# An fp32 trunk of two layers: the first steps of the MLPs' second products accumulate a sum on a copied PSUM bank, with a third bank in an opening and three order ties

## The chip, the cores and the metric

The kernel runs on one core of one Trainium2 chip. The metric is the device time of one execution, in microseconds (us), and the median of several runs stands for a kernel. The engines go by the profile's names: PE multiplies matrices, PEld loads PE's weights, DVE is the vector engine, ACT the scalar engine, POOL is GpSimd, and SP is the engine whose queue issues the DMAs. A lower time is better. The granted clock of PE was 1.000 in the profiled execution.

## The reference

The model is two layers over 1024 positions of width 1024. Layer 0 mixes positions with a chunked gating MLP, layer 1 with dilated attention. A dense MLP with a squared ReLU follows each mixer, and it is the two MLPs that the change touches:

```python
def reference(x, ...):
    h = x
    for layer in range(DEPTH):          # DEPTH = 2
        y = _rms_norm(h, mix_norm_g[layer])
        ...
            y = _chunk_gating_mixer(...)            # layer 0
        ...
            y = _dilated_attention_mixer(...)       # layer 1
        h = h + y
        y = _rms_norm(h, mlp_norm_g[layer])
        h = h + jnp.square(jax.nn.relu(y @ w_up[layer])) @ w_down[layer]
    return _rms_norm(h, final_norm_g)
```

`w_up` is 1024 x 4096 and `w_down` 4096 x 1024, all in float32.

## The kernel before

**Precision.** Each fp32 operand is split into two parts, hi and lo. `split` issues the hi part as an ACT copy (line 228) and the lo part as a DVE subtraction (line 229). A product of one block is three matmuls of 512 columns: hi by hi, hi by lo, lo by hi.

**Seven products.** Most MLP work goes as a two by two scheme with seven products instead of eight: sums and differences of the four quarters of the weights (POOL, lines 392 to 397, from four loaded quarters) meet sums and differences of the activations. They are numbered 1 to 7. A product may accumulate on what a PSUM bank already holds (the last argument `True` of `product`).

**Banks.** PSUM has eight banks in two pools: three `mm` banks (`mm_bank()`) and five `at` banks (`at_bank()`). A pool hands its banks out in turn, and a new use waits until the bank's last reader is done.

**Order.** PE's order is the order of the program. A scheduler orders the other engines' instructions by estimated times; `tc.issue_after(x)` around an instruction is a tie, which makes it come after `x` in that order. `more()` takes the next step of preparing the weights that come next.

**An MLP, in order.**

- `mlp` starts with a plain part for the first two column groups (`q` = 0, 1): for each half `s` of the positions, four tiles `n` each accumulate on a bank of their own over eight blocks. When a half is done, ACT empties the four banks with ReLU (line 863) and squares them (line 864).
- `opening` does `q` = 2 to 4 with the seven products, then come `q` = 5 to 15 in a form that copies a bank to another (`sums`) and accumulates there. Terms of the hidden activations go to DRAM (`hid`) in `kept`.
- `Down.run` does the second product in 18 steps `t`. Step `t` has 1, 2, 3 and then 4 blocks in each of its seven products, so 3, 6, 9 or 12 matmuls in each product for t = 0 to 3. `inputs` loads the hidden terms of the step after. `add` adds a finished bank to the residual `h` on DVE (line 1094). `self.u[a]` is the sum that several quarters need; it is kept until its last use in steps 14 to 17, where POOL adds it to `h`.
- In steps `t` < 4 ACT copies the first product's bank `a_` to SBUF as `u` (line 1112), the product 6 goes to an at bank `b`, and DVE adds it to `u` (line 1129). In the steps after that ACT copies `a_` to a second mm bank `sums` (line 1117), product 6 accumulates there, and DVE adds `sums` to `u` (line 1129).
- `Down.early` loads and splits the terms of the last column group, called in the step `q` = 15 of the first product.

**Layer 0 to layer 1.** `begin_attention` calls `value_weights(0)` for the attention's first value weights (line 1204) once layer 0's down product has emptied its last bank.

**The norm's terms.** `Terms.first` makes the normed blocks of the first half of the positions, `keep` (line 435), and `Terms.second` makes those of the second half (`r`, line 454) with differences to the first (`b`, lines 458 and 459). POOL writes two more in place (lines 460 and 461). `there[k]` is the event after which the planner may begin `second` for `k`.

Of the kernel before, what the change touches and what calls it, by code (L numbers as in the profile page):

```python
# [14 lines left out]
AF = mybir.ActivationFunctionType  # L15
ALU = mybir.AluOpType
# [113 lines left out]
def trunk(ctx: ExitStack, tc: tile.TileContext, xT, w_u, w_v, w_o, w_s, b_s, w_qkv, w_vt, w_bo, rel,  # L130
          w_up, w_dn, w_dl, vecs, gain, onehot, outT, outL):
    nc = tc.nc
# [12 lines left out]
    def temp():  # L145
        return tpool.tile([P, HALF], F32, tag="t", name="t")

    def spare():
        return tpool.tile([P, HALF], F32, tag="b", name="b", bufs=2)
# [41 lines left out]
    def mm_bank():  # L191
        return psm.tile([P, HALF], F32, tag="mm", name="mm")

    def at_bank():
        return psa.tile([P, HALF], F32, tag="at", name="at")
# [53 lines left out]

    KCOLS = [blk(k) for k in range(KT)]  # L250

    roots, scaled_by = [], []

    def rsqrt(src, scale, out=None, power_of=True):

# [104 lines left out]
    SEVEN = (1, 5, 7, 6, 2, 3, 4)  # L360
# [6 lines left out]
    def product(bank, w, xs, more=False):  # L367

        for k, x in enumerate(xs):
            three(bank, w, blk(k), x, not more and k == 0, k == len(xs) - 1, skip_group_check=True)  # L370
            flow.pump()
# [44 lines left out]
    class Terms:  # L416
# [25 lines left out]
        def second(self, sq, gi):  # L442
            yield from sq.sums()
            r = sq.rms()
            yield LAT["rms"]
            pb = spread(r)
            tt = nc.vector.tensor_tensor
            for k in range(4):
                yield self.there[k], 0
                y, x, (y0, y1) = [], [], (self.kept[k][:, j, :] for j in range(2))  # L450
                for j in range(2):
                    o = 4 * j + k
                    t = raw()
                    nc.vector.scalar_tensor_tensor(t, h[o][:, sq.cols], vec[:, gi, o:o + 1], pb, op0=ALU.mult, op1=ALU.mult)  # L454
                    y.append(t)
                    x.append(pair().split(t))
                t1, t2 = spare(), spare()
                tt(t1, y[0], y0, op=ALU.subtract)
                tt(t2, y[1], t1, op=ALU.subtract)
                nc.gpsimd.tensor_tensor(y0, y[1], y[0], op=ALU.subtract)  # L460
                nc.gpsimd.tensor_tensor(y1, y1, t2, op=ALU.subtract)
                yield 2 * LAT["tile"]
                for j in range(2):
                    self.blocks[j, 1].append(x[j])
                self.t[5].append(pair("t1").split(t1))
                self.t[6].append(pair("t2").split(t2))
# [279 lines left out]
    for gi, chunks in enumerate(((0, 1, 2), (3, 4, 5), (6, 7))):  # L746
        banks = {}
        for k in range(KT):
# [7 lines left out]
            with tc.issue_after(scaled_by[0] if k == 1 else gelus[5]) if gi == 1 and k else nullcontext():  # L756
                w = weight(w_v[k])
# [62 lines left out]
    for tiles in ((0, 1, 2), (3,), (4,), (5, 6, 7)):  # L820
        w = [weight(w_u[m]) for m in tiles]
        if tiles[0] == 3:
            flow.add(prepare(PREPARED[0], PACE[0]))
        for s in range(2):
            for i, m in enumerate(tiles):
                b = at_bank() if m > 2 and m % 2 else mm_bank()
# [9 lines left out]
    for tiles in ((0, 1), (2,), (3,), (4, 5, 6, 7)):  # L836
        w = [weight(w_o[m]) for m in tiles]
        for s in range(2):
            for i, m in enumerate(tiles):
                b = mm_bank()  # L840
# [39 lines left out]
    def mlp(layer, x, first, last, stored=None):  # L880
# [10 lines left out]
            hidden_terms(q, c[q, 0, 0], c[q, 1, 0], c[q, 0, 1], c[q, 1, 1], c[q, 0, 0])  # L891

        for s in range(2):
            banks = [at_bank() if (n < 2) == (s == 1) else mm_bank() for n in range(4)]
            if s == 0:
                banks = [mm_bank() if n < 3 else at_bank() for n in range(4)]
            order = [(j, k) for j in range(2) for k in range(4)] if s == 0 else [(j, k) for k in range(4) for j in range(2)]
            for n, (j, k) in enumerate(order):
                xs = x.blocks[j, s]
                flow.until(lambda: len(xs) > k)  # L900
                for b, (q, i) in zip(banks, tiles):
                    three(b, first[q][i, j], blk(k), xs[k], n == 0, n == 7)
                    flow.pump()
            for b, (q, i) in zip(banks, tiles):
                c[q, i, s] = temp()
                with tc.high_priority(offset=PRIO):
                    squared(c[q, i, s], b)
                if s and i and q == 0:
                    held_terms(q)
            if s == 0:  # L910
                w = up_weights(2)
                for _ in w.steps():
                    pass
# [56 lines left out]
        for q in range(2, 16):  # L970
            down = Down(layer) if q == 15 else None
            wn = down.weights(0) if down else up_weights(q + 1)
            forward, calls = ahead(wn), [0]

            def more():
                forward()
                calls[0] += 1
                if q >= OPEN and calls[0] in LATER:
                    save()
                    next(coming_late[layer], None)  # L980
                if q == 15 and calls[0] == 7:
                    save()

            more()
            if q < OPEN:
                c11, c21, c12, c22 = opening(q, w, more)
            else:
                a = at_bank()
                product(a, w[1], x.t[1])
                more()  # L990
                sums = mm_bank()
                with tc.high_priority(offset=PRIO):
                    nc.scalar.activation(sums, a, AF.Copy)
                if down:
                    down.take(14, held, SEVEN[:4])
                d = at_bank()
                product(d, w[5], x.t[5])
                more()
                c22 = temp()
                nc.scalar.activation(c22, d, AF.Copy)  # L1000
                if down:
                    down.take(14, held, SEVEN[4:])
                product(sums, w[6], x.t[6], True)
                more()
                c12 = temp()
                with tc.high_priority(offset=PRIO):
                    nc.scalar.activation(c12, sums, AF.Copy)
                if down:
                    down.early(SEVEN[:4])
                product(a, w[2], x.t[2], True)  # L1010
                more()
                c11 = temp()
                squared(c11, a)
                product(sums, w[7], x.t[7], True)
                more()
                nc.vector.tensor_tensor(c22, c22, sums, op=ALU.add)
                squared(c22)
                if down:
                    down.early(SEVEN[4:])
                product(d, w[3], x.t[3], True)  # L1020
                more()
                nc.vector.tensor_tensor(c12, c12, d, op=ALU.add)
                squared(c12)
                product(sums, w[4], x.t[4], True)
                c21 = temp()
                squared(c21, sums)
            if q < 14:
                hidden_terms(q, c11, c21, c12, c22, temp())
            elif q == 14:
                held = hidden_terms(q, c11, c21, c12, c22, temp(), False)  # L1030
            else:
                kept(q, {(0, 0): c11, (1, 0): c21, (0, 1): c12, (1, 1): c22})
            w = wn
# [3 lines left out]
    class Down:  # L1037
# [43 lines left out]
        def run(self, w):  # L1081
            for t, (a, ks) in enumerate(self.todo):
# [7 lines left out]
                def xs(p):  # L1090
                    return [self.x[self.order[k]][p] for k in ks]
# [4 lines left out]
                def then(evacuated, p):  # L1096

                    with tc.issue_after(evacuated) if t < 3 else nullcontext():
                        more()
                        self.inputs(t + 1, (p,))  # L1100
                    if self.layer == 0 and 5 <= t < 17 and p in STEPS:
                        save()
                        next(beside, None)
# [2 lines left out]
                    self.ends(0)  # L1106
                a_ = mm_bank()
                product(a_, w[1], xs(1))
                if t < 4:
                    self.u[a] = spare() if t < 2 else temp()  # L1110
                    more()
                    nc.scalar.activation(self.u[a], a_, AF.Copy)
                    self.inputs(t + 1, (1,))
                else:
                    more()
                    sums = mm_bank()
                    nc.scalar.activation(sums, a_, AF.Copy)  # L1117
                    self.inputs(t + 1, (1,))
                d = at_bank()
                product(d, w[5], xs(5))  # L1120
                then(add(1, 1, d), 5)
# [2 lines left out]
                then(add(1, 1, e), 7)  # L1124
                if t == 16:
                    self.ends(1)
                b = at_bank() if t < 4 else sums
                product(b, w[6], xs(6), t >= 4)
                then(nc.vector.tensor_tensor(self.u[a], self.u[a], b, op=ALU.add).ins, 6)
                product(a_, w[2], xs(2), True)  # L1130
                then(add(0, 0, a_), 2)
                product(d, w[3], xs(3), True)
# [67 lines left out]
    def begin_attention(sq, emptied):  # L1200
        s = sq.cols.start // HALF
        if s == 0:
            with tc.issue_after(emptied):
                firsts.extend(value_weights(0))
        flow.add((terms_a.second_plain if s else terms_a.first)(sq, 2), LAT["sum"])

# [94 lines left out]
    def more():  # L1301
        if next(coming, 1) == 1:
            next(ending, None)
# [749 lines left out]
```

## Time and profile before

| | |
|---|---|
| median of 3 runs | 2099.99 us (2097.24 to 2100.13) |
| profiled execution, its own time | 2096.62 us |
| its span | 2094.5 us |
| PE busy | 2081.9 us, 99% |
| PE's weight loads | 1722.9 us, 82% |
| DVE busy | 1543.7 us, 74% |
| ACT busy | 1165.3 us, 56% |
| POOL busy | 564.5 us, 27% |
| DMA | 387.36 MB, mean 185 GB/s |

The span is the stretch that the profiler saw, and the execution's own time is 2.1 us longer. A share is of the span. Times of single instructions are given from the span's start. Matmuls overlap: one is listed with 0.39 us, and the next one starts before it ends, so the pace is read from start to start. A figure in brackets behind a row is how long the engine stood idle before it, with the instruction whose end released it. The opening of layer 0's MLP is near 320 us, its down product begins near 610 us and ends near 893 us; the opening of layer 1's MLP is near 1480 us, and its down product begins near 1772 us.

### The profile page before, as it was taken

The numbers are of one execution on the slowest core, as the hardware profiler recorded it, in microseconds if no ns is written. First come the engines' busy times: TensorE is split into PE (matmuls) and PEld (weight loads), VectorE is DVE, ScalarE is ACT, GpSimd is POOL, SyncE is SP. The second block draws the span as 40 slices with busy tenths as digits, with TensorE's granted clock in tenths as the row PEclk, the third lists the DMA queues.
The fourth block names the chain that finished last, engine by engine and source line by source line (L and its number), as shares of the span: only waits on it lengthen the run. The fifth ranks groups of instructions, "written<-read, shape, count | busy, mean of one in ns | idle before, by whom it ended". The sixth has DMA issues, their size and how long they took to land.

```text
span 2094.5 us, 30757 instructions
## 1 busy us (share of the span) xinstructions
PE 2081.9 (99%) x10166; PEld 1722.9 (82%) x10166; DVE 1543.7 (74%) x2804; ACT 1165.3 (56%) x2367; POOL 564.5 (27%) x424
## 2 busy tenths in 40 slices
PE   9999999999999999999999999999999999999998
PEld 8888888888888888878888888888888888888887
DVE  7868769666689999878835665757985446988776
ACT  6535436566675555345556665776556556544443
POOL 2200124323324233430011212112532222433245
PEclk9999999999999999999999999999999999999999
DMA  6338814687765766643875656582256443654432
GB/s 232 123 95 293 305 38 141 197 280 276 259 222 192 232 215 226 231 166 135 309 216 159 182 163 185 170 274 81 91 196 202 149 151 127 205 166 155 148 120 86
DMA packets 224387, 387.36 MB, mean 185 GB/s; under 512 B 39913, under 2 KB 66660, under 8 KB 224228
## 3 DMA queue, kind: packets, MB, share of 16 engines
q1 hardware_dynamic: 215088, 384.03, 55.7%
q10 hardware_dynamic: 9140, 1.36, 0.4%
q8 instruction: 80, 1.31, 0.3%
q14 instruction: 79, 0.65, 0.1%
HBM read 252.50 MB, written 132.81 MB: 184 GB/s over the span
## 4 chain that ended last, share of the span: by engine, by line
PE 89%; DVE 5%; ACT 2%; DMA 2%; issue 1%; POOL 1%; SPq 0%; DVEq 0%; ACTq 0%; POOLq 0%
PE mm L198 44%; PE at L198 43%; PE at L205 2%; ACT t L1532 1%; DMA r<-in_w_v 1%; DVE hx L229 1%; DVE y L229 1%; DMA ex<-sc 0%; POOL t L292 0%; DVE tr L229 0%; ACT tr L228 0%; DMA r<-in_w_dn 0%; DVE wp L229 0%; DVE r L454 0%; DVE dn L1681 0%
## 5 line engine op out<-in xcount | busy, mean ns | idle before, releaser
L229 DVE TENSOR_TENSOR wp<-r,wp 128x512 fp32r<-128x512 f32 (+3 forms) x399 | 326.9, 825 | 120.1 <-ACT wp L228 118.0
L228 ACT ACTIVATE wp<-r 128x512 fp32r<-128x512 f32 (+3 forms) x399 | 236.1, 596 | 314.0 <-PE at L198 195.3
L198 PE MATMUL mm<-t,wp 128*128 128x512 f32 x1368 | 344.7, 395 | 0.1
L198 PE MATMUL at<-hx,wp 128*128 128x512 f32 x1452 | 340.9, 389 | 1.8 <-DVE h L1094 1.8
L198 PEld LDWEIGHTS at<-hx,wp 128*128 128x128 f32 x1452 | 272.1, 188 | 60.0 <-DVE h L1094 3.4
L198 PEld LDWEIGHTS mm<-t,wp 128*128 128x128 f32 x1368 | 250.8, 188 | 52.8 <-issue 0.7
L198 PE MATMUL at<-y,wp 128*128 128x512 f32 x1008 | 245.3, 389 | 0.0
L198 PE MATMUL mm<-hx,wp 128*128 128x512 f32 x984 | 234.2, 389 | 0.0
L198 PEld LDWEIGHTS at<-y,wp 128*128 128x128 f32 x1008 | 189.1, 188 | 39.5 <-issue 0.4
L198 PEld LDWEIGHTS mm<-hx,wp 128*128 128x128 f32 x984 | 184.6, 188 | 38.7 <-ACT mm L1117 0.4
L198 PE MATMUL mm<-y,wp 128*128 128x512 f32 x816 | 209.8, 396 | 1.1 <-DVE y L229 0.6
L392 POOL TENSOR_TENSOR t<-r 128x512 f32<-128x512 f32 (+3 forms) x62 | 81.1, 1308 | 476.6 <-DMA r<-in_w_up 141.0
L198 PEld LDWEIGHTS mm<-y,wp 128*128 128x128 f32 x816 | 149.2, 188 | 33.0 <-DVE y L229 1.0
L229 DVE TENSOR_TENSOR hx<-t,hx 128x512 fp32r<-128x512 f32 x192 | 163.1, 854 | 5.3 <-ACT hx L228 5.1
L292 POOL TENSOR_TENSOR t<-t 128x512 f32<-128x512 f32 (+1 forms) x62 | 78.2, 1263 | 247.0 <-ACT t L287 244.6
L394 POOL TENSOR_TENSOR r<-r 128x512 f32<-128x512 f32 (+3 forms) x62 | 91.0, 1468 | 168.8 <-DVE wp L229 156.7
L228 ACT ACTIVATE hx<-t 128x512 fp32r<-128x512 f32 x192 | 118.8, 627 | 26.0 <-DMA t<-hid 22.1
L198 PE MATMUL at<-t,wp 128*128 128x512 f32 x552 | 130.7, 389 | 0.0
L198 PE MATMUL mm<-y,whi 128*128 128x512 f32 x416 | 128.6, 390 | 0.0
L198 PEld LDWEIGHTS at<-t,wp 128*128 128x128 f32 x552 | 103.6, 188 | 21.5
L1094 DVE TENSOR_TENSOR h<-h,at 128x512 f32<-128x512 f32 x144 | 97.6, 679 | 25.7 <-PE at L198 25.4
L1532 ACT ACTIVATE t<-t,st 128x128 f32<-128x128 f32 (+1 forms) x192 | 84.3, 440 | 39.7 <-DVE st L1530 39.3
(262 smaller groups left out, 3517.4 us busy)
## 6 DMA issues: line engine op xcount, KB each, us to landing
t<-hid SPq DMA_DIRECT2D x182, 256.0 KB, 4.3
wd<-tr SPq DMA_DIRECT2D x154, 256.0 KB, 3.2
wp<-wd SPq DMA_DIRECT2D x77, 512.0 KB, 3.9
hid<-t SPq DMA_DIRECT2D x140, 256.0 KB, 3.0
r<-in_w_up SPq DMA_DIRECT2D x120, 256.0 KB, 2.9
r<-in_w_dn SPq DMA_DIRECT2D x80, 256.0 KB, 2.6
hid<-b SPq DMA_DIRECT2D x56, 256.0 KB, 3.0
r<-in_w_v SPq DMA_DIRECT2D x48, 256.0 KB, 3.3
```

The source lines that it names most:

```text
L198: nc.tensor.matmul(out, lhsT, rhs, **kw)
L205: nc.tensor.transpose(out, src, ident)
L228: return (nc.scalar.activation(hi, src, AF.Copy).ins, (engine or nc.vector).tensor_tensor(lo, src, hi.bitcast(F32), op=ALU.subtract).ins)
L229: (engine or nc.vector).tensor_tensor(lo, src, hi.bitcast(F32), op=ALU.subtract).ins)
L292: nc.gpsimd.tensor_tensor(self.acc, self.acc, sq, op=ALU.add)
L392: tt(r3, r[0, 0], r[1, 0], op=ALU.subtract)
L394: tt(r[1, 1], r[1, 0], r[0, 0], op=ALU.subtract)
L1094: return engine.tensor_tensor(hs[i, s], hs[i, s], src, op=ALU.add).ins
L1532: nc.scalar.activation(p[:, c], p[:, c], AF.Exp, bias=m, scale=-1.0, accum_out=dn)
```

## The change

Three things change, in both layers' MLPs.

1. **Steps t < 4 of `Down.run`.** `a_` is now copied to a second mm bank in these steps too, product 6 accumulates on that bank, and ACT copies the result out to `u` (line 1124 after). The DVE addition of these eight steps goes, the at bank `b` goes, and there are eight more ACT copies.
2. **The opening.** For `s` = 1 the tiles n = 0 to 2 take at banks (before: n = 0 and 1), and only n = 3 an mm bank.
3. **Three ties.** `second` waits for `there[3]` at every `k`, so all four blocks of the first half come first; the second part of `down.early` is tied behind the addition of line 1016; and the value weights are tied behind the last copy of `a_` in layer 0's `Down.run`, too.

```diff
-    roots, scaled_by = [], []
+    roots, scaled_by, copies = [], [], []
...
             for k in range(4):
-                yield self.there[k], 0
+                yield self.there[3], 0
...
-            banks = [at_bank() if (n < 2) == (s == 1) else mm_bank() for n in range(4)]
+            banks = [at_bank() if (n < 2 + s) == (s == 1) else mm_bank() for n in range(4)]
             if s == 0:
                 banks = [mm_bank() if n < 3 else at_bank() for n in range(4)]
...
-                nc.vector.tensor_tensor(c22, c22, sums, op=ALU.add)
+                added = nc.vector.tensor_tensor(c22, c22, sums, op=ALU.add).ins
                 squared(c22)
-                if down:
-                    down.early(SEVEN[4:])
+                with tc.issue_after(added) if down else nullcontext():
+                    down and down.early(SEVEN[4:])
...
                 a_ = mm_bank()
                 product(a_, w[1], xs(1))
-                if t < 4:
-                    self.u[a] = spare() if t < 2 else temp()
-                    more()
-                    nc.scalar.activation(self.u[a], a_, AF.Copy)
-                    self.inputs(t + 1, (1,))
-                else:
-                    more()
-                    sums = mm_bank()
-                    nc.scalar.activation(sums, a_, AF.Copy)
-                    self.inputs(t + 1, (1,))
+                more()
+                sums = mm_bank()
+                copies.append(nc.scalar.activation(sums, a_, AF.Copy).ins)
+                self.inputs(t + 1, (1,))
...
-                b = at_bank() if t < 4 else sums
-                product(b, w[6], xs(6), t >= 4)
-                then(nc.vector.tensor_tensor(self.u[a], self.u[a], b, op=ALU.add).ins, 6)
+                product(sums, w[6], xs(6), True)
+                if t < 4:
+                    self.u[a] = spare() if t < 2 else temp()
+                    summed = nc.scalar.activation(self.u[a], sums, AF.Copy)
+                else:
+                    summed = nc.vector.tensor_tensor(self.u[a], self.u[a], sums, op=ALU.add)
+                then(summed.ins, 6)
...
-            with tc.issue_after(emptied):
+            with tc.issue_after(emptied), tc.issue_after(copies[-1]):
                 firsts.extend(value_weights(0))
```

What this does to the order shows in three places. In the rows below a minus is the kernel before, a plus the one after. First, ACT at the start of layer 0's down product, steps t = 0 and 1 (`wp` are the parts of the weights, `hx` those of the hidden terms):

```order
 L228 ACTIVATE wp<-r 128x256
-L1112 ACTIVATE b<-mm 128x512
-L228 ACTIVATE wp<-r 128x256 x3
+L1111 ACTIVATE mm<-mm 128x512
+L228 ACTIVATE wp<-r 128x256 x2
+L1124 ACTIVATE b<-mm 128x512
+L228 ACTIVATE wp<-r 128x256
 L228 ACTIVATE wp<-t 128x256
 L228 ACTIVATE wp<-r 128x256
-L1112 ACTIVATE b<-mm 128x512
-L228 ACTIVATE wp<-r 128x384 x5
+L1111 ACTIVATE mm<-mm 128x512
```

The copy of `a_` keeps its place and goes to a bank; the copy out of the sum follows two weight splits later.

Second, ACT at the end of layer 0's down product. The rows `mm_8819<-mm_8812` are the copy of the last step, t = 17, and `wp_8971` to `wp_8986` are splits of the attention's value weights:

```order
 L228 ACTIVATE y_8794<-t_8688 128x256
+L1111 ACTIVATE mm_8819<-mm_8812 128x512
 L228 ACTIVATE wp_8971<-r_8972 128x512
 L228 ACTIVATE wp_8976<-r_8977 128x512
 L228 ACTIVATE wp_8981<-r_8982 128x512
 L228 ACTIVATE wp_8986<-r_8987 128x512
-L1117 ACTIVATE mm_8819<-mm_8812 128x512
```

The copy moves from behind the four splits to ahead of them.

Third, DVE in the opening of layer 1's MLP. `y<-keep` is the lo part of a block of the first half, `r` a block of the second half, `b`, `t1` and `t2` differences and their lo parts. Before, the last two lo parts of the first half stand among the second half's work:

```order
L229 TENSOR_TENSOR y_15323<-keep_15231,y_15323 128x512
L229 TENSOR_TENSOR t1_15332<-b_15307,t1_15332 128x512
L229 TENSOR_TENSOR t2_15335<-b_15308,t2_15335 128x512
L454 SCALAR_TENSOR_TENSOR r_15338<-h_14240,vec_80,at_15288 128x512
L454 SCALAR_TENSOR_TENSOR r_15343<-h_14282,vec_80,at_15288 128x512
L458 TENSOR_TENSOR b_15348<-r_15338,keep_15217 128x512
L229 TENSOR_TENSOR y_15340<-r_15338,y_15340 128x512
L229 TENSOR_TENSOR y_15345<-r_15343,y_15345 128x512
L459 TENSOR_TENSOR b_15349<-r_15343,b_15348 128x512
L229 TENSOR_TENSOR y_15358<-keep_15249,y_15358 128x512
```

After, they follow the last `keep` block almost at once:

```order
L435 SCALAR_TENSOR_TENSOR keep_15249<-h_14286,vec_80,at_15181 128x512
L229 TENSOR_TENSOR y_15307<-keep_15231,y_15307 128x512
L454 SCALAR_TENSOR_TENSOR r_15323<-h_14238,vec_80,at_15288 128x512
L229 TENSOR_TENSOR y_15320<-keep_15249,y_15320 128x512
L454 SCALAR_TENSOR_TENSOR r_15328<-h_14280,vec_80,at_15288 128x512
L229 TENSOR_TENSOR y_15325<-r_15323,y_15325 128x512
L458 TENSOR_TENSOR b_15333<-r_15323,keep_15186 128x512
```

The two lo parts moved up; the other instructions of this stretch are the same in kind and number. In SP's queue, four loads of the hidden terms (of products 6, 2, 3 and 4 of the step after) now stand behind one weight load in step t = 2 and behind two in step t = 3, in both layers.

## The prediction

> **What bounds the kernel now.** I read the busy times first, then the chain that ended last, then the table of what TensorE (PE) waited for, and last the timeline around each of those waits.
>
> ```profile
> PE 2081.9 (99%) x10166; PEld 1722.9 (82%) x10166; DVE 1543.7 (74%) x2804; ACT 1165.3 (56%) x2367; POOL 564.5 (27%) x424
> PE 89%; DVE 5%; ACT 2%; DMA 2%; issue 1%; POOL 1%; SPq 0%; DVEq 0%; ACTq 0%; POOLq 0%
> ```
>
> PE is busy for 99% of the span and carries 89% of the chain. The change leaves every matmul in place, so the number of matmuls times their pace stays. Only what PE waits can go, or come:
>
> ```profile
> PE at L198 <- DVE h L1094: 1.8, 2, 0.9
> PE idle L225 <- DVE scalars L216: 1.1, 1, 1.1
> PE mm L198 <- ACT mm L1117: 0.7, 1, 0.7
> PE mm L198 <- DVE y L229: 0.6, 1, 0.6
> ```
>
> The columns are total us, times, and the longest; these are its four largest rows. The change can reach three of them (all but the second), 3.1 us, and one wait of 0.45 shown next. So a few us are at stake. These idle times begin at a matmul's modelled end, so a stall is worth more than they say, and I measure it from start to start. The pace, and the first stall, in PE's timeline (start, duration, count):
>
> ```profile
> 316.19 2.20 PE L198 MATMUL mm<-y,wp 128*128 128x512 f32 x9
> 318.23 2.20 PE L198 MATMUL at<-y,wp 128*128 128x512 f32 x9
> 320.88 1.65 PE L198 MATMUL mm<-y,wp 128*128 128x512 f32 x6 [0.45 <-ACT t L863]
> ```
>
> Nine matmuls from 316.19 to 318.23 make 0.2267 us each. The next should start at 318.23 + 9 x 0.2267 = 320.27; it started at 320.88, 0.61 late. Six matmuls after a stall also take 1.65 - 0.39 = 1.26 us from first to last start, where 5 x 0.2267 = 1.13: a restart costs 0.1 more. So each stall is lateness plus 0.1.
>
> **A. The opening's third bank.** This is layer 0, second half of the positions: tiles n = 0, 1 use at banks, n = 2, 3 mm banks, which ScalarE must first empty.
>
> ```profile
> 320.24 1.56 ACT L863 ACTIVATE t<-mm 128x512 f32<-128x512 f32 x3
> ```
>
> The matmuls of n = 2 waited for the first of these three. Now n = 2 has a free at bank and runs 320.27 to 320.95, and n = 3 wants its mm bank at 320.95, when the emptying that let PE go at 320.88 is done. Gain 0.61 + 0.1 = 0.7. In layer 1 the same place shows no wait for L863; there it gains nothing.
>
> **B. Down's steps t = 0 to 3.** Each of eight steps loses one DVE addition (L1129) and gains one ACT copy; the copy of `a_` (L1112) now goes to a bank instead of SBUF. On ACT the eight extra copies are 8 x 0.59 = 4.7 us of an engine that is 56% busy; they cost nothing while its slack lasts, and without that slack they would delay the splits behind them (rival 3). On DVE one 0.68 us addition fewer stands ahead of what PE waits for at t = 2:
>
> ```profile
> 632.54 2.20 PE L198 MATMUL mm<-hx,wp 128*128 128x512 f32 x9
> 635.66 4.40 PE L198 MATMUL at<-hx,wp 128*128 128x512 f32 x18 [0.92 <-DVE h L1094]
> ```
>
> PE could go on at 632.54 + 2.04 = 634.58 and went at 635.66: 1.08, with the restart 1.2. It waited for the DVE addition at the end of these rows (DVE and, apart from them, POOL):
>
> ```profile
> 624.10 0.68 DVE L1129 TENSOR_TENSOR b<-b,at 128x512 f32<-128x512 f32 x1
> ...
> 629.84 1.06 DVE L229 TENSOR_TENSOR wp<-r,wp 128x384 fp32r<-128x384 f32 x1
> 630.82 1.77 DVE L229 TENSOR_TENSOR hx<-t,hx 128x512 fp32r<-128x512 f32 x1
> ...
> 634.93 0.68 DVE L1094 TENSOR_TENSOR h<-h,at 128x512 f32<-128x512 f32 x1
> ```
> ```profile
> 628.90 1.58 POOL L392 TENSOR_TENSOR t<-r 128x512 f32<-128x512 f32 x1 [5.14 <-DMA r<-in_w_dn]
> 630.56 1.49 POOL L393 TENSOR_TENSOR r<-r 128x512 f32<-128x512 f32 x1
> ```
> ```profile
> 1790.91 1.30 POOL L392 TENSOR_TENSOR t<-r 128x512 f32<-128x512 f32 x1 [5.79 <-DMA r<-in_w_dn]
> ```
>
> DVE has no gap there, so taking out 624.10's row moves all up by 0.60 (its 0.68 less the 0.08 by which an instruction overlaps the next, as 629.84 + 1.06 = 630.90 does 630.82), if nothing else holds DVE. Something does: where the addition of 512 columns at 624.10 takes 0.68, the split of 512 at 630.82 takes 1.77, ending 0.54 after POOL's 630.56 + 1.49 = 632.05, and the one at 629.84 ends 0.42 after POOL's 630.48. POOL started when a weight load landed, not when DVE did anything. With DVE 0.60 earlier, POOL's first starts against a DVE addition from a bank and may take 1.30, as it does in layer 1 (the third row), instead of 1.58, which puts the pair 0.28 earlier; the rest of the 0.60 is lost in waiting. So the row gives 0.3, the plain shift 0.6. I take 0.3, since both long rows are exactly there. The Trainium skill, "SBUF — State Buffer", section "SBUF: two separate sides", says that the vector engine with two SBUF inputs and GpSimd take one port pair in turn, the later one blocked until the other's instruction ends. By that rule this term would be 0.3, without it 0.6; these rows agree with the rule.
>
> The same place in layer 1, on DVE and PE (POOL's row stands above):
>
> ```profile
> 1791.21 1.42 DVE L229 TENSOR_TENSOR wp<-r,wp 128x384 fp32r<-128x384 f32 x1
> 1792.55 1.78 DVE L229 TENSOR_TENSOR hx<-t,hx 128x512 fp32r<-128x512 f32 x1
> ```
> ```profile
> 1794.29 2.20 PE L198 MATMUL mm<-hx,wp 128*128 128x512 f32 x9
> 1797.39 1.88 PE L198 MATMUL at<-hx,wp 128*128 128x512 f32 x7 [0.90 <-DVE h L1094]
> ```
>
> Here the stall is 1797.39 - 1796.33 = 1.06, with restart 1.2. With DVE 0.60 earlier the first split starts at 1790.61, before POOL's 1790.91; then only one of the two is held, and DVE gains 0.60 plus part of the 1.1 that a held split costs. I take it that the DVE end no longer binds here.
>
> What PE meets earlier in the same step series, at t = 0, is new. The third product now goes on the copied bank, so it waits for the copy:
>
> ```profile
> 610.61 2.20 PE L198 MATMUL at<-hx,wp 128*128 128x512 f32 x9
> 612.64 0.84 PE L198 MATMUL mm<-hx,wp 128*128 128x512 f32 x3
> ```
> ```profile
> 611.75 0.59 ACT L1112 ACTIVATE b<-mm 128x512 f32<-128x512 f32 x1
> ```
>
> At t = 0 a product is three matmuls. The third of the three at products in the first row starts at 610.61 + 6 x 0.2267 = 611.97; the copy in that place of ACT's order ends at 612.34, and PE starts about 0.05 after a release (634.93 + 0.68 against 635.66). New wait 0.42, with restart 0.5, and I take the same in layer 1. At t = 1 to 3 two products of 6 to 12 matmuls (2.7 to 5.4 us) lie between, so no wait.
>
> That new wait does not add where DVE's end binds later, since DVE does not move with PE. Layer 0: PE leaves t = 2 when DVE lets it, 0.3 earlier than before. Bounds 0 and 0.6. Layer 1: the stall of 1.2 goes, the new 0.5 comes: 0.6 after rounding. Bounds 0 and 0.7.
>
> **C. The tie of the value weights.** End of layer 0's down product, t = 17:
>
> ```profile
> 888.13 1.52 PE L198 MATMUL mm<-hx,y 128*128 128x512 f32 x6
> 889.49 2.88 PE L198 MATMUL at<-hx,y 128*128 128x512 f32 x12
> 893.04 1.20 PE L198 MATMUL mm<-hx,y 128*128 128x512 f32 x4 [0.66 <-ACT mm L1117]
> ```
> ```profile
> 890.55 1.95 ACT L228 ACTIVATE wp<-r 128x512 fp32r<-128x512 f32 x3 [6.08 <-DMA r<-in_w_vt]
> 892.40 0.58 ACT L1117 ACTIVATE mm<-mm 128x512 f32<-128x512 f32 x1
> ```
>
> PE should start at 889.49 + 12 x 0.2267 = 892.21 and started at 893.04: 0.83, with restart 0.9. The copy stood behind three splits that waited 6.08 us for a load. Now it stands ahead of them, and its source is done at 889.65: it ends near 890.3, 1.9 before it is needed. Gain 0.9. The splits behind it lose at most 0.58, and they wait for the load until 890.55 anyway.
>
> **D. The tie in the layer 1 opening.** The lo parts for k = 2, 3 of the first half go ahead of the second half's work on DVE.
>
> ```profile
> 1479.49 0.39 PE L198 MATMUL mm<-y,wp 128*128 128x512 f32 x1
> 1480.50 1.67 PE L198 MATMUL mm<-y,wp 128*128 128x512 f32 x6 [0.62 <-DVE y L229]
> ```
> ```profile
> 1503.57 3.67 PE L198 MATMUL mm<-y,wp 128*128 128x512 f32 x14
> ```
> ```profile
> 1479.77 0.68 DVE L229 TENSOR_TENSOR y<-keep,y 128x512 fp32r<-128x512 f32 x1
> ```
> ```profile
> 1464.00:1506.00 42.00, 41.35 (x183) 33.59 (x184) 39.56 (x54) 21.59 (x39) 19.34 (x11) 1.00 0.15 51
> ```
>
> PE stood from 1479.72 to 1480.50, 0.8, for the split at 1479.77, which now runs some 9 us earlier. That stall goes. But in the row at 1503.57 fourteen matmuls should take 13 x 0.2267 + 0.39 = 3.34 and take 3.67: PE waits again at the end of a DVE chain, which is busy 39.56 of 42 us (third figure of the windows row). The tie reorders the same DVE work and removes none, so PE comes 0.9 earlier to the same gate and waits there instead. Net 0; between -1.1 (one more split held by POOL, 1.77 against 0.68) and +1.2 (both stalls go). I take 0, as the chain's length is what decides.
>
> The third tie, of the held terms after L1016, moves an addition up on DVE at the end of the up product, where no row shows PE waiting: 0.
>
> **Sum.** A 0.7 + B 0.3 + 0.6 + C 0.9 + D 0 = 2.5 us. The profiled execution of 2096.62 (its span of 2094.5 and 2.1 around it) would take 2094.1. It lies 3.4 under the median of the runs shown, 2099.99, which themselves reach from 2097.24 to 2100.13; the difference taken from the median gives 2097.5. That is 0.12%, under the 0.2% (4.2 us) that a measurement of this kernel tells from no change.
>
> **Rivals.**
> 1. The layer 1 chain shortens. For it: two splits there leave the middle of the POOL-held stretch. Against it: DVE does the same work. D becomes +1.2, total 3.7 and up to 4.0 with B at its upper bounds: 2096.1.
> 2. The waits are only traded. B gives nothing, D loses 1.1: total 0.7 + 0.9 - 1.1 = 0.5, so 2099.5. For it: the new wait at t = 0 and POOL's hold; against it: DVE's removed row is real.
> 3. Slower: SyncE's queue, steps t = 2 and 3. The change puts weight loads ahead of four loads of hidden terms; each weight load waits for a buffer that DVE's splits free, and the four wait behind it.
>
> ```profile
> 646.41 3.27 SPq L187 DMA_DIRECT2D t<-hid  x7
> 651.87 6.80 SPq L187 DMA_DIRECT2D r<-in_w_dn  x3
> ```
>
> Four of the seven that went out from 646.41 now go after the second of those three, perhaps 8 us later, and ACT and DVE take their splits in order. It decides once the splits behind them come after PE's turn; then PE stands for about a product, 12 x 0.2267 = 2.7 us, in each layer: +5.4 - 2.5 = +2.9, 2102.9. Against it: the loads belong to the step after the one that runs, and a step of t = 3 is seven products, 19 us, so even 8 us late they come in time.
> 4. Nothing is gained: each stall reappears whole one step on. Against it: in C the next matmuls depend on PE alone. 2100.0.
>
> **Chances.** Forecast (gain 1.5 to 3.3) 0.45, rival 1 0.2, rival 2 0.2, rival 3 0.08, rival 4 0.07. The likeliest case alone lies between 2096.7 and 2098.5. The range takes in rivals 1, 2 and 4 and, as medians of three scatter over 2.9 us, goes lower by most of that: 2094.6 to 2100.4. Faster by over 0.2% needs rival 1 and a low median: 0.15. Slower by over 0.2% is rival 3 at more than its price: 0.05. Within: 0.80.
>
> **What would show it.** After: no wait for L863 near 320; a wait of the mm product for the ACT copy near 612 and 1773, about 0.4 each; the t = 2 wait for L1094 shorter in layer 0 and gone in layer 1; none for the copy at 892; none for y near 1480, but a longer one near 1505. The forecast is wrong if PE's waits for ACT grow at t = 1 to 3, or if a wait for hx splits appears at t = 3 or 4.

## The result, and the profile after

Over 14 runs each, the changed kernel's median is 2095.02 us (2092.06 to 2097.72) and that of the kernel before 2097.71 us (2095.75 to 2100.5). The ratio is 0.9986, with a 95% interval of 0.9979 to 0.9992: 1.7 to 4.4 us of gain are compatible with it, and 2.7 is the middle. The prediction had 2.5. The time itself came out 2.5 below the forecast of 2097.5, because the median of the kernel before, 2099.99 over the 3 runs that were known, is 2097.71 over 14.

The profiled execution's span is 2094.0 us, only 0.5 less than before. This is no contradiction: the first 300 us, which the change doesn't touch, lost 1.8 us more to PE stalls in this trace. Single traces are therefore compared place by place here. PE's busy time is the same as before, DVE has 12 us less to do, and the table of PE's waits has another first row:

```profile
PE 2082.0 (99%) x10166; PEld 1722.7 (82%) x10166; DVE 1531.6 (73%) x2796; ACT 1167.3 (56%) x2375; POOL 563.0 (27%) x424
```
```profile
PE mm L198 <- ACT mm L1111: 1.6, 2, 1.4
...
PE at L198 <- DVE h L1094: 0.3, 1, 0.3
```

The wait for L1094 fell from 1.8 to 0.3 us, the waits for L863, L1117 and y are gone, and 1.6 us of a new one came: PE for the copy of `a_`. PE's timeline shows where. In the opening of layer 0 (A) the start after nine matmuls is on pace now, 318.34 + 2.04 = 320.38, and it is an at bank:

```profile
318.34 2.20 PE L198 MATMUL mm<-y,wp 128*128 128x512 f32 x9
320.38 2.88 PE L198 MATMUL at<-y,wp 128*128 128x512 f32 x12
```

At t = 0 of `Down.run`, first layer 0, then layer 1 (B), product 6, the fourth of the step, waits:

```profile
612.10 1.52 PE L198 MATMUL at<-hx,wp 128*128 128x512 f32 x6
614.99 1.20 PE L198 MATMUL mm<-hx,wp 128*128 128x512 f32 x4 [1.37 <-ACT mm L1111]
```
```profile
1771.66 1.52 PE L198 MATMUL at<-hx,wp 128*128 128x512 f32 x6
1773.45 1.65 PE L198 MATMUL mm<-hx,wp 128*128 128x512 f32 x6 [0.27 <-ACT mm L1111]
```

Six matmuls take 1.36, so PE is 1.53 late in layer 0 and 0.43 in layer 1, each with 0.1 for the restart. At t = 2 PE is on pace in both layers; layer 1's rows, where 18 matmuls last 4.08:

```profile
1791.94 4.24 PE L198 MATMUL mm<-hx,wp 128*128 128x512 f32 x18
1796.03 4.39 PE L198 MATMUL at<-hx,wp 128*128 128x512 f32 x18
```

In layer 1 the prediction had only one of the two splits held by POOL. Both still are, 1.26 and 1.77 us long:

```profile
1790.02 1.26 DVE L229 TENSOR_TENSOR wp<-r,wp 128x384 fp32r<-128x384 f32 x1
1791.20 1.77 DVE L229 TENSOR_TENSOR hx<-t,hx 128x512 fp32r<-128x512 f32 x1
```
```profile
1789.57 1.30 POOL L392 TENSOR_TENSOR t<-r 128x512 f32<-128x512 f32 x1 [5.03 <-DMA r<-in_w_dn]
```

What moved is POOL's start. The load that it waits for goes out when a DVE split has freed the buffer. SP's wait before (1786 to 1788 us), and that split before and after:

```profile
SPq L187 <- DVE wp L229: 0.8, 1, 0.8
```
```profile
1786.67 0.55 DVE L229 TENSOR_TENSOR wp<-r,wp 128x384 fp32r<-128x384 f32 x1
```
```profile
1785.48 0.55 DVE L229 TENSOR_TENSOR wp<-r,wp 128x384 fp32r<-128x384 f32 x1
```

From that split's end to POOL's start are 1790.91 - 1787.22 = 3.69 us before and 1789.57 - 1786.03 = 3.54 after. The removed addition stood ahead of the split, so its 0.60 moved the load and POOL, too: from the end of the DVE split ahead of the addition's place to the end of this one are 1.68 us before and 1.08 after.

But at t = 3 of layer 1 a stall is new. 24 matmuls last 5.44, so PE should have started at 1813.86 and did at 1814.29. It waited for a DVE addition that now stands behind two splits of the next step, and these end with POOL's sums (1809.78 + 1.61 = 1811.39 and 1811.47 + 1.62 = 1813.09):

```profile
1808.42 5.60 PE L198 MATMUL mm<-hx,wp 128*128 128x512 f32 x24
1814.29 3.04 PE L198 MATMUL at<-hx,wp 128*128 128x512 f32 x12 [0.27 <-DVE h L1094]
```
```profile
1810.16 3.48 DVE L229 TENSOR_TENSOR hx<-t,hx 128x512 fp32r<-128x512 f32 x2
1813.56 0.67 DVE L1094 TENSOR_TENSOR h<-h,at 128x512 f32<-128x512 f32 x1
```
```profile
1809.78 1.61 POOL L394 TENSOR_TENSOR r<-r 128x512 f32<-128x512 f32 x1 [0.70 <-DVE wp L229]
1811.47 1.62 POOL L397 TENSOR_TENSOR r<-r 128x512 f32<-128x512 f32 x1
```

At t = 17 of layer 0 (C) the copy goes right after its source and the next product keeps pace (890.60 + 2.72 = 893.32):

```profile
890.60 2.88 PE L198 MATMUL at<-hx,y 128*128 128x512 f32 x12
893.32 2.88 PE L198 MATMUL mm<-hx,y 128*128 128x512 f32 x12
```
```profile
890.80 0.58 ACT L1111 ACTIVATE mm<-mm 128x512 f32<-128x512 f32 x1 [7.05 <-PE mm L198]
```

In layer 1's opening (D) the stall near 1480 is gone, and the one near 1505 is larger: five matmuls from 1503.03 should last 1.13 and take 1.70. That is 0.57 late, 0.68 with the restart that follows, instead of 0.30.

```profile
1503.03 1.55 PE L198 MATMUL mm<-y,wp 128*128 128x512 f32 x5
1504.73 2.57 PE L198 MATMUL mm<-y,wp 128*128 128x512 f32 x10 [0.15 <-DVE wp L229]
```

### The profile page after: what moved, and what is told of

It is laid out like the page before. It is cut to its first block, busy times and chain, and to the rows that moved or that the text cites. A ratio compares the mean times of both kernels' runs of the same rounds, so it can differ in the third digit from the quotient of the medians.

```text
span 2094.0 us, 30761 instructions
## 1 busy us (share of the span) xinstructions
PE 2082.0 (99%) x10166; PEld 1722.7 (82%) x10166; DVE 1531.6 (73%) x2796; ACT 1167.3 (56%) x2375; POOL 563.0 (27%) x424
## 3 DMA queue, kind: packets, MB, share of 16 engines
q10 hardware_dynamic: 9140, 1.36, 0.4%
q8 instruction: 80, 1.31, 0.3%
## 4 chain that ended last, share of the span: by engine, by line
PE 87%; DVE 6%; DMA 3%; ACT 3%; issue 1%; POOL 1%; SPq 0%; DVEq 0%; ACTq 0%; POOLq 0%
PE mm L198 44%; PE at L198 41%; PE at L205 2%; DMA r<-in_w_v 1%; ACT t L1532 1%; DMA h<-in_xT 1%; POOL t L292 1%; DVE wlo L229 1%; DVE tr L229 0%; DMA ex<-sc 0%; DVE t L229 0%; DVE hx L229 0%; DVE y L229 0%; DVE wp L229 0%; ACT tr L228 0%
## 5 line engine op out<-in xcount | busy, mean ns | idle before, releaser
L229 DVE TENSOR_TENSOR wp<-r,wp 128x512 fp32r<-128x512 f32 (+3 forms) x399 | 313.6, 791 | 129.2 <-ACT wp L228 127.8
L198 PE MATMUL at<-hx,wp 128*128 128x512 f32 x1392 | 326.9, 389 | 0.3 <-DVE h L1094 0.3
L198 PEld LDWEIGHTS at<-hx,wp 128*128 128x128 f32 x1392 | 261.1, 188 | 55.3 <-DVE h L1094 1.1
L198 PE MATMUL at<-y,wp 128*128 128x512 f32 x1056 | 256.2, 389 | 0.0
L198 PE MATMUL mm<-hx,wp 128*128 128x512 f32 x1044 | 247.9, 389 | 1.6 <-ACT mm L1111 1.6
L198 PEld LDWEIGHTS at<-y,wp 128*128 128x128 f32 x1056 | 198.1, 188 | 41.4 <-issue 0.3
L198 PEld LDWEIGHTS mm<-hx,wp 128*128 128x128 f32 x1044 | 195.8, 188 | 43.0 <-ACT mm L1111 2.5
L198 PE MATMUL mm<-y,wp 128*128 128x512 f32 x768 | 198.7, 396 | 0.2 <-DVE wp L229 0.2
L229 DVE TENSOR_TENSOR hx<-t,hx 128x512 fp32r<-128x512 f32 x192 | 169.3, 887 | 14.0 <-ACT hx L228 13.5
L198 PEld LDWEIGHTS mm<-y,wp 128*128 128x128 f32 x768 | 140.2, 188 | 29.9 <-DVE wp L229 0.6
L1094 DVE TENSOR_TENSOR h<-h,at 128x512 f32<-128x512 f32 x144 | 97.7, 679 | 23.6 <-PE at L198 23.2
```

The lines of the kernel that those rows point to most:

```text
L198: nc.tensor.matmul(out, lhsT, rhs, **kw)
L229: (engine or nc.vector).tensor_tensor(lo, src, hi.bitcast(F32), op=ALU.subtract).ins)
L1094: return engine.tensor_tensor(hs[i, s], hs[i, s], src, op=ALU.add).ins
```

## The experiments

Each trace gives a table of what PE lost at the places of the change: the sum of all lateness from start to start (over 0.2267 us, if more than 0.025, after matmuls of 512 columns), restarts included, in us. The first four columns have the old order at most places, the last four all or part of the new one. The names are those of the runs below.

| place | before | e2 bank | e3 second | e4 values | after | e5 again | e1 sum | e9 no accum. |
|---|---|---|---|---|---|---|---|---|
| first 300 us, untouched | 2.97 | 4.03 | 3.47 | 4.33 | 4.81 | 4.65 | 3.46 | 3.42 |
| A, layer 0 opening, 300 to 340 | 0.81 | 0.23 | 0.90 | 0.91 | 0.22 | 0.22 | 0.91 | 0.22 |
| B, layer 0, q = 15's end to t = 1 | 0.00 | 0.43 | 0.26 | 0.35 | 1.64 | 0.67 | 2.36 | 1.33 |
| B, layer 0, t = 2 | 1.33 | 1.64 | 1.43 | 1.65 | 0.03 | 0.65 | 0.18 | 1.68 |
| B, layer 1, t = 0 to 3 | 1.17 | 1.31 | 0.97 | 0.99 | 1.19 | 0.94 | 0.54 | 1.64 |
| C, end of layer 0, 870 to 900 | 1.55 | 2.71 | 0.51 | 1.18 | 0.00 | 0.40 | 1.18 | 0.57 |
| D, layer 1 opening, 1440 to 1520 | 1.85 | 1.85 | 1.33 | 1.89 | 1.33 | 1.35 | 1.89 | 1.33 |

Between the columns before and after, the four places gain 0.6 (A), -0.4 (B), 1.6 (C) and 0.5 (D), together 2.3; less the 1.8 of the first 300 us that is the 0.5 of the spans. In A, 0.1 between the columns is a restart that falls inside or outside the edge at 300.

**One part alone.** Each kernel is the one before with one hunk of the diff. A single run's time can't tell parts of under 1 us, so these four ran once each: 2097.96 (e1), 2099.62 (e2), 2096.02 (e3) and 2097.98 us (e4), beside 2099.21 for the kernel before.

The accumulation:

```diff
...
+                sums = mm_bank()
+                nc.scalar.activation(sums, a_, AF.Copy)
...
+                product(sums, w[6], xs(6), True)
+                if t < 4: ... nc.scalar.activation(self.u[a], sums, AF.Copy)
```

> The kernel before with the accumulation in steps t = 0 to 3 alone; no third bank, no ties. Theory: PE waits about 0.4 us at t = 0 of each layer for the copy of a_, loses the t = 2 waits of 1.1, and keeps the other stalls of the kernel before (0.6 at 320, 0.8 at 892, 0.8 at 1480). In layer 0 the part is then worth +0.3 to +0.6, in layer 1 at most 0.1, since the wait of 0.4 seen at t = 3 of the changed kernel comes with it. Rival: the 1.5 us wait at t = 0 of layer 0 in the changed kernel belongs to the accumulation alone; then it shows here too and layer 0 loses 0.3.

The t = 0 waits were 0.43 in both layers, and the t = 2 waits went. So the 1.53 of the changed kernel does not belong to the accumulation alone. But layer 0 lost more just ahead of it, at the end of q = 15, to an addition that stood behind splits of late loads:

```profile
PE mm L198 <- DVE t L1016: 1.5, 1, 1.5
```

So layer 0 lost 1.2 us where the theory had a gain of 0.3 to 0.6. Layer 1 gained 0.63 where it had 0.1 at most, as no wait came at t = 3. That is the prediction's own 0.6 for layer 1.

The bank:

```diff
-            banks = [at_bank() if (n < 2) == (s == 1) else mm_bank() for n in range(4)]
+            banks = [at_bank() if (n < 2 + s) == (s == 1) else mm_bank() for n in range(4)]
```

> The kernel before with the opening's third at bank alone. Theory: the 0.6 us stall near 320 goes, all others stay as before, 0.7 us shorter. Rival: n = 3 waits for its mm bank instead, so a stall of 0.2 or more shows one tile later.

For the stall near 320 the theory held: its 0.61 and the restart went, and one tile later 0.04 came. But the others did not stay as before. Place C lost 2.71 instead of 1.55, and 0.43 came at the end of q = 15, both behind loads.

The tie of the second half's terms:

```diff
-                yield self.there[k], 0
+                yield self.there[3], 0
```

> The kernel before with the tie of the second half's terms alone. Theory of the prediction: the 0.8 us stall near 1480 goes and comes back whole near 1505 (0.3 becomes 1.2), net 0. Rival, as the changed kernel's trace has it: the chain of DVE work itself gets shorter and the stall near 1505 is about 0.5 to 0.7, net 0.5 to 0.6 shorter.

The rival held. Place D loses 1.33 instead of 1.85, in this kernel and to within 0.02 in each of the traces above with that tie. (Of the three further kernels with it, below, e7 loses 1.58 there, with 0.38 late for a weight split of ACT where the others have 0.12 to 0.15.) The same stretch near 1505:

```profile
1502.79 2.23 PE L198 MATMUL mm<-y,wp 128*128 128x512 f32 x8
1505.18 2.12 PE L198 MATMUL mm<-y,wp 128*128 128x512 f32 x8 [0.15 <-DVE wp L229]
```

The chain did not lose an instruction, but it lost holding time. Where POOL runs its sums (lines 460 and 461), DVE's two-input instructions are long. Before, first, and after, second, at the start of that stretch:

```profile
1475.22 1.72 DVE L458 TENSOR_TENSOR b<-r,keep 128x512 f32<-128x512 f32 x1
1477.47 1.77 DVE L229 TENSOR_TENSOR y<-r,y 128x512 fp32r<-128x512 f32 x1
```
```profile
1474.30 1.12 DVE L229 TENSOR_TENSOR t<-b,t 128x512 fp32r<-128x512 f32 x1
1475.35 0.73 DVE L454 SCALAR_TENSOR_TENSOR r<-h,vec,at 128x512 f32<-128x512 f32 x1
1476.00 1.13 DVE L229 TENSOR_TENSOR y<-r,y 128x512 fp32r<-128x512 f32 x1
```
```profile
1474.83 1.75 POOL L461 TENSOR_TENSOR keep<-keep,b 128x512 f32<-128x512 f32 x1
```

The last row is POOL's after. Now an instruction of line 454, which has a bank as an input and is not held (0.73 to 0.74), stands where POOL begins, and only the rest of POOL's sum holds the next one. Summed over the long instructions from 1474 to 1499, the excess over 0.68 is 8.1 us after and 8.6 us before: 0.5, the gain of D. Counted from 3 us ahead of POOL's first sum of lines 460 and 461 to the end of its last, the excess is 6.39 to 6.41 in the six traces with the old order and 5.88 to 5.90 in the seven with the tie.

The tie of the value weights:

```diff
...
-            with tc.issue_after(emptied):
+            with tc.issue_after(emptied), tc.issue_after(copies[-1]):
```

> The kernel before with the tie of the value weights alone. Theory: the 0.8 us stall near 892 goes with its restart, 0.9 shorter, and the small stalls at 881 to 887 (together 0.6) stay. Rival, as the changed kernel has none of the small stalls either: they come from the same queue order and go with it, 1.5 to 1.7 shorter.

The stall at t = 17 is gone, and the small ones at t = 15 and 16 stay, as the theory had it; with restarts they are 1.18 here and were 0.61 in the profile before. But the stall at t = 17 is also absent or nearly so, without the tie, in four other traces: with restart it was 0.93 in the profile before and 1.42 in e2, 0.15 in e1, and zero in e3, e10 and e11. The splits stood ahead of the copy there, too, but the load of the value weights landed 2.5 to 3.4 us ahead of PE's turn, against 1.8 and 1.3 in the two traces with the stall. With the tie it is absent in all seven traces.

**The change once more, and undoing parts.** The next four ran on one chip, five rounds each.

> The changed kernel once more, for a second trace and as the reference of this chip. Theory: waits that PE has for DVE or ACT work behind a DMA (near 613 in layer 0, at t = 3 of layer 1) differ from trace to trace, since the loads land at other times; the stalls with no DMA behind them (none at 320 and 1480, 0.4 to 0.45 at t = 0 of layer 1, 0.7 in sum near 1504) come again within 0.05. Ratio 0.998 to 0.9995. Rival: the 1.5 near 613 is fixed by the order and shows again within 0.2.

Ratio 0.9988 (0.9979 to 0.9997). The theory held: A, D and the 0.43 at t = 0 of layer 1 came again within 0.02, while the 1.53 near 613 became 0.56 and the t = 3 wait of layer 1 was absent. But waits at t = 2 came, 0.54 late in layer 0 and 0.29 in layer 1. The cause of the spread near 613 shows on ACT, in the changed kernel's first trace and then in the second:

```profile
607.71 0.63 ACT L228 ACTIVATE hx<-hr 128x512 fp32r<-128x512 f32 x1 [1.52 <-DMA hr<-hid]
...
611.47 0.63 ACT L863 ACTIVATE t<-t 128x512 f32<-128x512 f32 x1 [0.63 <-DVE t L1022]
...
614.36 0.58 ACT L1111 ACTIVATE mm<-mm 128x512 f32<-128x512 f32 x1
```
```profile
606.00 0.63 ACT L228 ACTIVATE hx<-hr 128x512 fp32r<-128x512 f32 x1 [0.92 <-DMA hr<-hid]
```

ACT first waits for a load of the held terms; DVE splits them and only then adds in line 1022; ACT waits for that, and five more instructions stand between that one and the copy of `a_`. How late the load lands sets how late the copy is.

```diff
...
-                with tc.issue_after(added) if down else nullcontext():
-                    down and down.early(SEVEN[4:])
+                if down:
+                    down.early(SEVEN[4:])
```

> The changed kernel without the tie of the held terms behind line 1016. Theory: the tie is worth something, against the prediction's 0: PE waits 1 to 1.8 us near 608 for the addition of line 1016, as with the accumulation alone, and then 0.4 at t = 0, so this is 0.3 to 1.0 us slower than the changed kernel (ratio 0.0002 to 0.0005 higher). Rival, the prediction: no difference at 608, and only 0.4 at t = 0, so 1.1 faster.

Ratio 0.9989 (0.998 to 0.9998), the same as the changed kernel within the intervals. The wait for line 1016 came back (0.75 late) and the t = 0 wait was 0.43: 1.40 together where the tie has 1.64 and 0.67. So the tie moves the wait from 608 to 613. Whether it gains anything stays open (the medians are 2098.05 without it and 2096.26 with it). This trace also has a wait at t = 4, near 668. PE was 1.31 late there for the copy of `a_`, which stood behind a split whose hidden term landed late:

```profile
668.07 0.63 ACT L228 ACTIVATE hx<-t 128x512 fp32r<-128x512 f32 x1 [1.29 <-DMA t<-hid]
668.61 0.61 ACT L228 ACTIVATE wp<-r 128x512 fp32r<-128x512 f32 x1
669.13 0.58 ACT L1111 ACTIVATE mm<-mm 128x512 f32<-128x512 f32 x1
```

```diff
+                with tc.high_priority(offset=PRIO) if t == 0 else nullcontext(): copies.append(...)
```

> The changed kernel with the copy of a_ at t = 0 given priority on ACT, so that it stands ahead of a squaring and a weight split (0.9 us). Theory: the wait at t = 0 goes in layer 1 (0.54 with restart to 0) and is 0.9 shorter in layer 0 (1.6 to 0.7, or 0 where the loads land early), 1.0 to 1.5 us faster than the changed kernel, ratio to before 0.998. Rival: what follows is bound by DVE, so the t = 2 waits return by as much and nothing is won.

Both t = 0 waits went to zero, and the kernel was not faster but about as slow as the one before: ratio 0.9999 (0.999 to 1.0008), median 2098.78 beside 2096.26 for the changed kernel on this chip. The rival held, and more: PE's wait moved to DVE, and the priority also moved DVE's order. From t = 0 to t = 4 PE lost 2.54 in layer 0 and 2.33 in layer 1, with 1.58 of it late at t = 3 of layer 1.

```profile
PE at L198 <- DVE h L1094: 3.1, 5, 1.4
```

```diff
-                    with tc.issue_after(evacuated) if t < 3 else nullcontext():
+                    with tc.issue_after(evacuated) if t < 4 else nullcontext():
```

> As the one with the copy first, and at t = 3 too the next loads and splits are tied behind the step's own evacuations (t < 4 instead of t < 3). Theory: the 0.54 at t = 3 of layer 1 goes as well; another 0.5 faster than with the copy first alone. Rival: the splits of the next step come later and PE waits for those at t = 4, nothing won.

Ratio 0.9994 (0.9986 to 1.0003). PE lost 1.68 in layer 0 and 2.35 in layer 1, together still more than the changed kernel's 2.86 for both (first trace) or 2.26 (second). The wait at t = 3 turned into others up to t = 4. Neither is a better version.

**Undoing the accumulation.** The changed kernel with t < 4 as before, five rounds, on another chip:

> The changed kernel with the steps t = 0 to 3 as before (DVE addition, at bank); bank and ties stay. The title's part is then worth the difference. Theory: little. The waits at t = 0 go (0.54 each), the t = 2 waits come back (1.2 to 1.6 in layer 0, 1.0 to 1.3 in layer 1), so 0.3 to 0.9 us slower than the changed kernel, ratio to before 0.9988 to 0.9993. Rival: the t = 2 waits are no longer than what the changed kernel loses at t = 0 and 3, same time as the changed kernel or faster.

Ratio 0.9988 (0.9979 to 0.9997), the same as with the accumulation: the timed gain is there without the title's part, too, and the intervals are too wide to tell a part of about 1 us. Its trace has the t = 2 waits again (1.08 and 1.53 late). But the wait at t = 0 of layer 0 did not go, 1.22 late. So the long wait near 613 needs no accumulation: here PE wants the bank of `a_` itself for the product after, and the same late copy holds it.

```profile
606.26 0.63 ACT L228 ACTIVATE hx<-hr 128x512 fp32r<-128x512 f32 x1 [1.87 <-DMA hr<-hid]
```
```profile
613.59 0.96 PE L198 MATMUL mm<-hx,wp 128*128 128x512 f32 x3 [1.05 <-ACT b L1112]
```

**What holds DVE at t = 2.** Two kernels that leave out work, one run each, both from the kernel before. The first:

```diff
...
-                then(nc.vector.tensor_tensor(self.u[a], self.u[a], b, op=ALU.add).ins, 6)
+                then(nc.vector.tensor_tensor(self.u[a], self.u[a], b, op=ALU.add).ins if t != 1 else was, 6)
```

> The kernel before without the DVE addition of step t = 1 in both layers (the sum u lacks that product). It takes 0.6 us out of DVE's work ahead of the t = 2 wait and puts no wait at t = 0. Theory (POOL holds DVE): the t = 2 stall of layer 0 shrinks by 0 to 0.3, not by 0.6, and the split that follows POOL's second sum still ends 0.55 after it; in layer 1 it shrinks by 0.6 or more if POOL holds one split fewer. Rival (plain shift): 0.6 shorter in both layers.

```profile
628.82 1.33 DVE L229 TENSOR_TENSOR wp<-r,wp 128x384 fp32r<-128x384 f32 x1
630.07 1.77 DVE L229 TENSOR_TENSOR hx<-t,hx 128x512 fp32r<-128x512 f32 x1
```
```profile
628.43 1.31 POOL L392 TENSOR_TENSOR t<-r 128x512 f32<-128x512 f32 x1 [5.09 <-DMA r<-in_w_dn]
629.81 1.48 POOL L393 TENSOR_TENSOR r<-r 128x512 f32<-128x512 f32 x1
```

The pair of held splits ends 631.84 - 628.43 = 3.41 after POOL's start, where it was 632.59 - 628.90 = 3.69 before: 0.28 won of the 0.60 taken out, as the theory had it. (POOL's start itself did not gain here: its load went out 0.8 earlier against the split ahead of the removed addition, and took as much longer.) The stalls at t = 2 shrank by more, to 0.07 and 0.19, because the scheduler also moved the addition that PE waits for ahead of a split (0.60); stalls of 0.42 and 0.44 came at t = 3. So neither the 0 to 0.3 of the theory nor the 0.6 of the rival can be read from the stalls; the held pair can be read.

```diff
...
-            tt(r3, r[0, 0], r[1, 0], op=ALU.subtract)
-            tt(r[1, 0], r[1, 0], r[1, 1], op=ALU.add)
+            bare or tt(r3, r[0, 0], r[1, 0], op=ALU.subtract)
+            bare or tt(r[1, 0], r[1, 0], r[1, 1], op=ALU.add)
...
```

> The kernel before without POOL's first two weight sums for step t = 3 in both layers (those products use unsummed weights). DVE's own instructions ahead of the t = 2 wait stay the same in number, kind and order. Theory (POOL holds DVE): the two long splits there take 0.55 and 0.68 instead of 1.06 and 1.77, DVE is 1.6 us earlier, and the t = 2 stall of 1.06 is gone in both layers. Rival: the splits are long for another reason, such as a late load or DVE's own queue, and the stall stays.

```profile
627.62 0.67 DVE L1129 TENSOR_TENSOR b<-b,at 128x512 f32<-128x512 f32 x1
...
633.36 0.54 DVE L229 TENSOR_TENSOR wp<-r,wp 128x384 fp32r<-128x384 f32 x1
633.83 0.68 DVE L229 TENSOR_TENSOR hx<-t,hx 128x512 fp32r<-128x512 f32 x1
...
636.84 0.67 DVE L1094 TENSOR_TENSOR h<-h,at 128x512 f32<-128x512 f32 x1
```

The same two splits take 0.54 and 0.68, and the addition comes 636.84 - 627.62 = 9.22 after L1129 instead of 634.93 - 624.10 = 10.83, 1.61 earlier. The theory is shown: POOL's sums hold DVE here. PE's stall for that addition went, and 0.84 and 0.56 came at the next product, whose addition now stood behind two splits that POOL's third and fourth sums held.

## Why the prediction was right or wrong, point by point

The total, 2.5 us for 2.7 measured, came out of terms that were off in both directions, so that it came so near is in part luck. The 2.9 us by which its range goes lower is the scatter of three runs, not of medians of three.

- **A**, 0.7: right. In every trace with the bank the 0.61 near 320 and its restart of 0.11 are gone, and 0.04 came behind.
- **B, the new wait at t = 0**, 0.42: right in layer 1 (0.43 in each of four traces), wrong in layer 0. The step took the copy to keep the place on ACT's clock that its row of before had. It keeps its place in the order, but that order hangs on a load, and PE was 0.43 to 1.53 late there. So "That new wait does not add where DVE's end binds later" fails in the first trace: 1.64 lost at t = 0 is more than the 1.33 that DVE had cost at t = 2, and PE, not DVE, was last. e7 took the wait away and gained nothing, but its DVE order had moved as well.
- **B, t = 2, layer 0**, 0.3: POOL's hold was right. From POOL's start to the end of the held pair are 3.41 us in both traces of the changed kernel, as in e10, and 3.69 before: 0.28. PE was on pace at t = 2 in the first trace and 0.54 late in the second.
- **B, t = 2, layer 1**, 0.6: the wait nearly went (0.11 and 0.40 with restart), but not by the step given. That "only one of the two is held" is wrong, both are; and "POOL started when a weight load landed, not when DVE did anything" leaves out that this load had waited for DVE. A t = 3 wait of 0.54 came in one of two traces. That was named as a sign of error for hx splits at t = 3 or 4, and the price was left out of the sum.
- **B in all**: from the end of q = 15 to t = 4 PE lost in both layers 2.86 and 2.26 with the change, 3.08 in e1 and 3.65 in e6 (1.42 of it at t = 4), and 2.50, 3.38, 2.66, 2.99 and 4.65 without the accumulation: means of 2.96 and 3.24. So the title's part is worth about 0.3 us by the traces, where the sum had 0.9. The two groups overlap, so even its sign is not shown, and e9's time does not resolve it.
- **C**, 0.9: the mechanism was right, the size that of one trace. Without the tie the wait was 0.93, 1.42, 0.15 and three times 0, a mean of 0.4.
- **D**, 0: wrong. The failed step is "The tie reorders the same DVE work and removes none, so PE comes 0.9 earlier to the same gate". The work was the same, but its length also holds POOL's share, and that fell by 0.5. It lay within the bounds given. This is rival 1, the shorter chain, at under half of its 1.2. (With B at its upper bounds that rival adds up to 4.1, not to the 4.0 given.)
- **The third tie**, 0: no gain is shown. PE's wait for line 1016, absent in the profile before, was there in six other traces without the tie (0.15 late in e3, 0.23 in e4, 0.32 in e2 and in e11, 0.75 in e6, 1.71 in e1), and the tie moves it on to the copy of `a_`.
- Rival 3 (SyncE's queue): no wait of its size came. Its mechanism shows in e6, which has the changed kernel's queue order there: 1.31 late at t = 4 behind a late hidden term, half of the 2.7 for a layer.

With these sizes the sum is 0.7 + 0.3 + 0.4 + 0.5 = 1.9 us, inside what the intervals of the two timings allow (1.7 to 4.4, and 0.6 to 4.4 in e5). How the rest of the 2.7 splits, or whether it is scatter, stays open.

## What to carry to other kernels

When the bottleneck engine is 99% busy, list its late starts from start to start and ask of each whether a load stands behind it: those with none came again within 0.06 us in the table's traces, those with one ranged from 0 to 1.7, and one trace is no average. A wait that is taken off PE gains only up to the next engine's backlog. Before taking a load's landing as given, look for what its issue waits for: here it was the very DVE chain that had been shortened. Reordering alone can shorten a DVE chain, as it did here by 0.5, if instructions that POOL doesn't hold are put where POOL starts.

## What the runs showed of the hardware that was not expected

- A held split ends a fixed time after POOL's instruction: 0.41 to 0.42 us for 384 columns and 0.54 to 0.56 for 512, in the kernel before, the changed one and e10; alone they take 0.54 and 0.68. The row at 1791.21 ends at 1792.63, and POOL's at 1790.91 ends at 1792.21. That DVE is held at all until POOL's instruction ends is the rule that the prediction cites from the Trainium skill, "SBUF — State Buffer", section "SBUF: two separate sides", and e11 bears it out: without POOL's sums the splits took 0.54 and 0.68.
- A load of 256 KB that is issued in the same place of the queue made ACT wait 0.71, 0.92, 1.52 and 1.87 us in four traces (the profile before, e5, the changed kernel, e9). Where the splits of such a load stand in order ahead of an instruction that PE needs, that scatter becomes PE's.
